# Transposing normalized keys and queries two units at a time, in halves of 64 rows, in a hybrid decoder layer

## The chip, the cores and the metric

The kernel runs on one core of a Trainium2 chip. The metric is the device time of one execution in microseconds. A core has TensorE (PE; its weight loads are listed apart as PEld), VectorE (DVE), ScalarE (ACT), GpSimd (POOL) and SyncE (SP), which here only issues DMAs. Each engine works through its own list of instructions in order; semaphores hold an instruction back until another engine or a DMA is done.

## The reference

One layer on x (2048 tokens, width 1024): an adaptive norm, one projection to queries, keys, values, forget logits and three conv inputs, attention of 8 heads of 64 beside a short gated convolution, an output projection, and a convolutional feed-forward part. What the change touches is the part that makes queries and keys:

```python
h = rmsnorm(x, norm1_g) * (1 + sc1) + sh1
proj = h @ w_in
q, k, v, fg, xin, bg, cg = jnp.split(proj, IN_SPLITS, axis=-1)
q = rmsnorm(q.reshape(b, s, ATTN_HEADS, HEAD_DIM), q_norm_g)
k = rmsnorm(k.reshape(b, s, ATTN_HEADS, HEAD_DIM), k_norm_g)
```

Keys and queries are wanted later with the head dimension on the partitions, so each normalized block of 128 tokens by 512 columns has to be transposed. They are also wanted as a pair of fp16 numbers, a high part and the rest (the low part), because products are made from three fp16 products.

## The kernel before

The work runs in stages: values and modulation, keys, queries, the conv inputs, attention with the output projection, and the feed-forward part. The change lies in the stage of keys and queries, `project` (L618). `project` is called for keys (L812) and then for queries (L814). Each call goes through 16 units of 128 tokens. I call them K0 to K15 and Q0 to Q15.

In a unit TensorE makes 24 matmuls of 128x512 (eight steps k of three fp16 products, `mm3`, L145) into a PSUM tile `acc`. ACT squares it (L649), DVE sums the squares per head and makes the reciprocal root (L651, L652, `rsqrt`), and DVE writes the normalized block `qn` (L655) to SBUF. `qn` goes onto a list, `normed`.

`finish(i, qn)` (L620) does the rest for one unit. TensorE transposes the block in four pieces of 128x128 fp32 (L623) into one PSUM tile `pt` of 512 columns. ACT scales and copies it to `tf` (L629), POOL makes the fp16 high part `th` (`pool_copy`, L139), DVE the low part `tl` (L631), and SP issues two stores to DRAM (L633). `finish` is called behind the last matmuls of a unit (`k == MID`, MID is 7) when three units are on the list, so it handles the block of three units earlier. The three units that are left at the end of a call are finished by `finish_last`: those of the keys as hooks of Q0, Q1 and Q2, those of the queries inside the first conv chunk (L854), one after each of the products x, c and b.

All PSUM tiles of this kind come from one pool, `ps_t`, with the tag `tr` and **two buffers**, taken in turn. Other small products take tiles of the same tag: the running offset `po` (L542, hook of K4), the scale of a weight group (`power_of_two`, a transpose at L173 and a matmul at L179, called from `next(group)` behind the last matmuls of a unit), `largest_value` and `value_scale` (L579, L584), and the modulation columns `pm` (L691, from `piece`, a hook of Q3, Q6, Q9, Q12 and Q15). The wrapper `K` keeps an instruction in program order on its engine. All TensorE instructions named here are wrapped, so on TensorE they stand just where the program has them: a small product that follows `finish` stands right behind its transposes, ahead of the next unit's matmuls. The other engines' lists are ordered by a scheduler.

During the queries a value tile is also split per unit (`value_tile`, L592): SP loads `vt` (L595), ACT and DVE make its high and low part `vo` (L600, L601), and SP stores them. `magnitudes` (L728) streams weights of the feed-forward part through ACT (L732). In SBUF, `tf` and `vt` share a tag with two buffers, and `th` and `vo` share another.

Of the kernel before, what the change touches and what calls it, by code (L numbers as in the profile page):

```python
# [20 lines left out]
P = 128  # L21
# [25 lines left out]
def kernel(  # L47
# [104 lines left out]
    with ExitStack() as ph:  # L152
# [438 lines left out]

        def value_tile(i):  # L592

            vt = bp.tile([P, AW], F32, tag="tf", name="vt")
            nc.sync.dma_start(vt, v_sc[i * P : (i + 1) * P, :])  # L595

            def split():
                vo = bp.tile([P, H, P], F16, tag="th", name="vo")
                v3 = vt.rearrange("p (h d) -> p h d", d=DH)
                A.activation(vo[:, :, 0:DH], v3, AF.Copy, scale=vs)  # L600
                V.scalar_tensor_tensor(vo[:, :, DH:P], v3, vs, vo[:, :, 0:DH], op0=ALU.mult, op1=ALU.subtract)  # L601
                nc.sync.dma_start(
                    v16_sc[:, i * P : (i + 1) * P, :, :].rearrange("r p a d -> p r a d"),
                    vo.rearrange("p (r a) d -> p r a d", a=2),
                )

            return split
# [7 lines left out]
                splits.append(value_tile(i))  # L615


        def project(w, units, col, gain, dst_hi, dst_lo, hooks, lull, group):  # L618

            def finish(i, qn):  # L620
                pt = ps_t.tile([P, 512], F32, tag="tr", name="pt")
                for j in range(4):
                    K(T.transpose(  # L623
                        pt[:, j * P : (j + 1) * P], qn[:, 2 * j : 2 * j + 2, :].rearrange("p h d -> p (h d)"), ident
                    ))
                tf = bp.tile([P, 512], F32, tag="tf", name="tf")
                th = bp.tile([P, 512], F16, tag="th", name="th")
                tl = bp.tile([P, 512], F16, tag="tl", name="tl")
                A.activation(tf, pt, AF.Copy, scale=gain)  # L629
                pool_copy(th, tf)  # L630
                V.tensor_tensor(tl, tf, th, op=ALU.subtract)  # L631
                for dst, src in ((dst_hi, th), (dst_lo, tl)):
                    nc.sync.dma_start(dst[:, :, i * P : (i + 1) * P], src.rearrange("p (j n) -> p j n", j=4))  # L633

            normed = []
            for i in range(NT):
                ch, t = divmod(i, 4)
                acc = ps_m.tile([P, 512], F32, tag="mm", name="acc")
                for k in range(KD):
                    ah, al = h_hi[k][ch][:, t * P : (t + 1) * P], h_lo[k][ch][:, t * P : (t + 1) * P]  # L640
                    mm3(acc, ah, al, w[k][0], w[k][1], k == 0, k == KD - 1)
                    if k == 3 and lull[0] <= i < lull[1]:
                        magnitudes()
                    if k == MID and len(normed) == 3:
                        finish(*normed.pop(0))
                next(group)
                a3 = acc.rearrange("p (h d) -> p h d", d=DH)
                sq = bp.tile([P, 512], F32, tag="z", name="sq")
                A.activation(sq, acc, AF.Square)  # L649
                r = bp.tile([P, 16], F32, tag="r", name="r")[:, 0:H]  # L650
                V.tensor_reduce(r, sq.rearrange("p (h d) -> p h d", d=DH), axis=AX.X, op=ALU.add)  # L651
                V.tensor_scalar(r, r, 1.0 / DH, units[1], op0=ALU.mult, op1=ALU.add)  # L652
                rsqrt(bp, r, H, "rq")
                qn = bp.tile([P, H, DH], F32, tag="qn", name="qn", bufs=4)
                V.tensor_tensor(qn, a3, r.unsqueeze(2).broadcast_to([P, H, DH]), op=ALU.mult)  # L655
                normed.append((i, qn))
                if i in hooks:
                    hooks[i]()
                if col == 0:
                    value_tiles(i)  # L660
                if lull[0] <= i < lull[1]:
                    magnitudes()

            def finish_last():
                finish(*normed.pop(0))
                if col == 0 and not normed:
                    value_tiles(NT)

            return finish_last
# [141 lines left out]
        w_q, u_q, group = columns_of(0, "wl")  # L811
        last_k = project(w_k, u_k, AW, gq[:, 1:2], k_hi, k_lo, {0: largest_gains, 1: gain_scales, 3: running_sum, 4: running_offset, 7: largest_value, 9: value_scale}, (0, 13), group)  # L812
        convs = [conv_group(0)]
        last_q = project(w_q, u_q, 0, gq[:, 0:1], q_hi, q_lo, {0: last_k, 1: last_k, 2: last_k, 3: piece, 6: piece, 9: piece, 12: piece, 15: piece}, (2, 15), convs[0][2])  # L814

        def load_head(h):

# [16 lines left out]
        for j in range(4):  # L834
# [5 lines left out]
            for ch in range(4):  # L840
# [7 lines left out]
                for name in ("x", "c", "b"):  # L848
                    pr[name] = ps_m.tile([P, 512], F32, tag="mm", name="pr")
                    for k in range(KD):  # L850
                        wh, wl = w[name][k // 4]
                        mm3(pr[name], wh[:, k % 4, :], wl[:, k % 4, :], h_hi[k][ch], h_lo[k][ch], k == 0, k == KD - 1)
                        if (j, ch, k) == (0, 0, MID):
                            last_q()  # L854
                    if j < 3 or (ch, name) == (0, "x"):
                        magnitudes()
# [16 lines left out]
                    next(scales)  # L873
                bt = bp.tile([P, 512], F32, tag="qn", name="bt", bufs=4)
                A.activation(bt, pr["b"], AF.Copy, scale=inv)
                y = bp.tile([P, 512], F32, tag="tf", name="y")
                cw = [cst[:, 72 + 4 * m + j : 73 + 4 * m + j] for m in range(3)]
                G.tensor_scalar(y, z[:, 0:512], cw[0], None, op0=ALU.mult)
                V.scalar_tensor_tensor(y, z[:, 1:513], cw[1], y, op0=ALU.mult, op1=ALU.add)
# [913 lines left out]
```

## Time and profile before

| what | value |
|---|---|
| median of 3 runs | 2374.75 us (2369.72 to 2375.34) |
| the profiled execution | 2379.02 us |
| its span in the trace | 2377.3 us |
| mean granted TensorE clock | 0.994 |
| transposes of the change's stage (L623), 128 of them | from 176.1 to 354.2 us |
| TensorE busy in the whole span | 96% |

The span is the time from the first to the last instruction; 1.7 us of the profiled execution lie around it. In the rows of the views, PE is TensorE's matmul side and PEld its weight loads. A form such as `128*128 128x512` gives rows and columns of the array in use, then the output's partitions by columns. A matmul's recorded duration holds its way through the array, so consecutive matmuls overlap in the record: their cost to TensorE is the distance between their starts. The idle time ahead of an instruction stands in brackets with what ended it.

### The profile page before, as it was taken

The page shows a single profiled execution, that of the slowest core. Times are in us where ns is not written, and L with a number is a line of the kernel's source. Part 1 is how long each engine was busy: PE and PEld are TensorE (multiplying, and loading weights), DVE is VectorE, ACT ScalarE, POOL GpSimd, SP SyncE. Part 2 cuts the span into 40 slices and gives each one's busy share as a digit, 9 for nine tenths or more (in the row PEclk, how much of TensorE's full clock was granted, in tenths as well). Part 3 has the DMA queues.
Part 4 walks back from the last instruction along what each step waited for, and adds up shares of the span by engine and source line. Part 5 has one row for each costly group of instructions (what it writes and reads, how often), then busy time and mean ns, then how long its engine had stood idle before and what let it go on. Part 6 is the DMA issues. An engine that isn't in the chain of part 4 may idle for free.

```text
span 2377.3 us, 38568 instructions
## 1 busy us (share of the span) xinstructions
PE 2277.8 (96%) x14208; PEld 1359.0 (57%) x14208; DVE 1740.6 (73%) x3404; ACT 1163.9 (49%) x1990; POOL 339.0 (14%) x282
## 2 busy tenths in 40 slices
PE   5899999999899898999999999999999999999998
PEld 5764554444677676444444444678764444447886
DVE  6768886673999887456999999766955566566556
ACT  5745543320788887343556556465522232224332
POOL 0211111111677784001000000000000000000000
PEclk9999999999999999999999999999999999999999
DMA  9346699963899997434465556676654444446665
GB/s 285 135 156 174 165 263 300 299 214 84 164 182 190 196 188 150 166 111 168 169 216 196 207 210 215 235 235 224 224 185 161 145 158 147 150 164 209 220 204 194
DMA packets 452646, 455.25 MB, mean 191 GB/s; under 512 B 191248, under 2 KB 301160, under 8 KB 451432
## 3 DMA queue, kind: packets, MB, share of 16 engines
q1 hardware_dynamic: 445336, 435.94, 62.0%
q10 hardware_dynamic: 4752, 8.46, 1.0%
q0 software_dynamic: 2368, 8.39, 0.9%
q8 instruction: 111, 1.82, 0.3%
q14 instruction: 79, 0.65, 0.1%
HBM read 284.84 MB, written 134.28 MB: 176 GB/s over the span
## 4 chain that ended last, share of the span: by engine, by line
PE 78%; DVE 11%; DMA 4%; ACT 4%; issue 2%; SPq 1%; POOL 0%; DVEq 0%; ACTq 0%
PE acc L1591 28%; PE acc L1748 14%; PE acc L145 13%; PE pr L145 10%; PE pv L145 2%; PE pt L1107 2%; PE ps L1046 1%; DMA far<-wide 1%; PE ps L1047 1%; DVE near L1114 1%; PE po L1143 1%; DVE s_t L1070 1%; ACT s_t L1087 1%; PE po L1145 1%; PE po L1144 1%
## 5 line engine op out<-in xcount | busy, mean ns | idle before, releaser
L1591 PEld LDWEIGHTS <-pair 128*128 128x128 f16 x3696 | 361.5, 98 | 439.7 <-issue 5.0
L1591 PE MATMUL acc<-t,pair 128*128 128x512 f16 x2112 | 477.3, 379 | 1.9 <-DVE t L1426 1.9
L1591 PE MATMUL acc<-b,pair 128*128 128x512 f16 x1584 | 363.4, 379 | 0.0
L1515 DVE TENSOR_TENSOR lo<-raw,hi 128x1024 fp32r<-128x1024 f32 x154 | 186.8, 1223 | 137.5 <-ACT hi L1514 128.3
L1604 DVE SCALAR_TENSOR_TENSOR w<-w,fcw,w 128x1024 f32<-128x1024 f32 x176 | 226.1, 1285 | 79.4 <-ACT w L1599 73.2
L1514 ACT ACTIVATE hi<-raw 128x1024 fp32r<-128x1024 f32 x154 | 160.9, 1056 | 188.7 <-PE acc L1748 136.4
L1748 PE MATMUL acc<-lo,hi 128*128 128x512 f32 x616 | 242.9, 394 | 7.3 <-DVE lo L1515 7.2
L1748 PE MATMUL acc<-hi 128*128 128x512 f32 x616 | 244.8, 397 | 5.4 <-DVE u L1426 3.6
L1748 PE MATMUL acc<-hi,lo 128*128 128x512 f32 x616 | 242.3, 393 | 0.0
L145 PEld LDWEIGHTS <-h 128*128 128x128 f16 x1344 | 130.3, 98 | 97.5 <-DVE h L358 5.4
L1599 ACT ACTIVATE w<-w,fcw 128x1024 f32<-128x1024 f32 x88 | 100.6, 1143 | 160.7 <-DVE w L1426 160.7
L145 PE MATMUL acc<-wp,mp 128*128 128x512 f16 x768 | 171.1, 382 | 1.1 <-DVE raw L999 1.0
L1087 ACT ACTIVATE s_t<-s_t,nb,cst 128x2048 f32<-128x2048 f32 (+15 forms) x128 | 164.7, 1288 | 4.8
L1099 POOL TENSOR_TENSOR wide<-s_t,wide 128x1024 f16<-128x1024 f32 x64 | 136.8, 2137 | 5.3
L1748 PEld LDWEIGHTS acc<-lo,hi 128*128 128x128 f32 x616 | 117.1, 190 | 33.3 <-DVE lo L1515 9.5
L1748 PEld LDWEIGHTS acc<-hi 128*128 128x128 f32 x616 | 117.0, 190 | 32.4 <-DVE u L1426 5.7
L1070 DVE CUSTOM_DVE_ANT_0 s_t<-ps,nf,mx 128x512 f32<-128x512 f32 (+1 forms) x192 | 119.4, 643 | 16.5 <-PE ps L1049 8.2
L1748 PEld LDWEIGHTS acc<-hi,lo 128*128 128x128 f32 x616 | 117.1, 190 | 24.9
L145 PE MATMUL pr<-h,wh 128*128 128x512 f16 x576 | 126.5, 379 | 0.0
L145 PEld LDWEIGHTS <-mp 128*128 128x128 f16 x768 | 75.3, 98 | 88.9 <-issue 3.5
L145 PE MATMUL pr<-h,wl 128*128 128x512 f16 x576 | 125.8, 379 | 0.0
L1046 PE MATMUL ps<-kh,qs 128*128 128x512 f16 (+1 forms) x320 | 109.6, 347 | 5.5 <-DVE mx L1070 4.5
(362 smaller groups left out, 4084.8 us busy)
## 6 DMA issues: line engine op xcount, KB each, us to landing
up_sc<-pair SPq DMA_DIRECT2D x132, 256.0 KB, 2.7
pair<-up_sc SPq DMA_DIRECT2D x132, 256.0 KB, 3.0
wx<-in_w_up_dram SPq DMA_DIRECT2D x88, 256.0 KB, 3.6
raw<-in_w_up_dram SPq DMA_DIRECT2D x44, 512.0 KB, 3.7
y_t<-t SPq DMA_DIRECT2D x88, 256.0 KB, 2.6
raw<-y_t SPq DMA_DIRECT2D x88, 256.0 KB, 3.9
raw<-w_sc SPq DMA_DIRECT2D x88, 256.0 KB, 4.4
y_b<-y SPq DMA_DIRECT2D x66, 256.0 KB, 2.0
```

The source lines that it names most:

```text
L145: ins = T.matmul(acc, lhsT=a, rhs=b, start=st, stop=sp)
L1046: K(T.matmul(ps[:, 0:cw], lhsT=qt, rhs=kh[:, c0 : c0 + cw], start=True, stop=False))
L1070: K(V.tensor_tensor_reduce(out=s_t[:, o0 + c0 : o0 + c0 + cw], in0=ps[:, 0:cw], in1=nf[:, c0 : c0 + cw], scale=1.0, scalar=-3.0e38 if g == ...
L1087: K(A.activation(cols, cols, AF.Exp, bias=nb[:, p : p + 1], scale=qk[:, 4:5], accum_out=un["l"][:, p : p + 1]))
L1099: K(G.tensor_tensor(wide[:, 1, :], s_t[:, WB * P : WU], wide[:, 0, :], op=ALU.subtract))
L1107: K(T.transpose(pt[:, b * P : (b + 1) * P], s_t[:, (b0 + b) * P : (b0 + b + 1) * P], ident))
L1514: K(A.activation(hi, raw, AF.Copy))
L1515: K(V.tensor_tensor(lo, raw, hi.bitcast(F32), op=ALU.subtract))
L1591: K(T.matmul(acc, lhsT=a, rhs=b, start=st, stop=sp, skip_group_check=True))
L1599: K(A.activation(y, u[:, 0:1024], AF.Copy, scale=fcw[:, ct : ct + 1]))
L1604: K(V.scalar_tensor_tensor(y, u[:, m : m + 1024], fcw[:, m * 44 + ct : m * 44 + ct + 1], y, op0=ALU.mult, op1=ALU.add))
L1748: K(T.matmul(acc[t], lhsT=a[:, c], rhs=b, start=st, stop=sp, skip_group_check=True))
```

## The change

`finish` takes two blocks, of units i and i+1, at once. Each 128x128 transpose becomes two, one of the upper and one of the lower 64 tokens: 64 rows of `qn` by 128 columns against a 64x64 part of the identity. The upper halves go to one PSUM tile and the lower halves to another, so a call takes both buffers of `tr`. That is 16 transposes of 128x64 where there were two times four of 128x128. ACT copies in four pieces of 256 columns, and the copy, the low part and the two stores then run once on 1024 columns. `finish` is called when four units are on the list (K4, K6 to K14, and the same for Q); the two last pairs of the keys are finished behind the matmuls of Q0 and Q1 (`others`), those of the queries behind the products x and c. `tf` and `tl` have one buffer, `vt` gets a tag of its own with one buffer, and the conv stage's `y` takes the tag `th`.

```diff
--- before.py
+++ after.py
@@ -591,7 +591,7 @@
 
         def value_tile(i):
 
-            vt = bp.tile([P, AW], F32, tag="tf", name="vt")
+            vt = bp.tile([P, AW], F32, tag="vt", name="vt", bufs=1)
             nc.sync.dma_start(vt, v_sc[i * P : (i + 1) * P, :])
 
             def split():
@@ -615,22 +615,30 @@
                 splits.append(value_tile(i))
 
 
-        def project(w, units, col, gain, dst_hi, dst_lo, hooks, lull, group):
-
-            def finish(i, qn):
-                pt = ps_t.tile([P, 512], F32, tag="tr", name="pt")
-                for j in range(4):
-                    K(T.transpose(
-                        pt[:, j * P : (j + 1) * P], qn[:, 2 * j : 2 * j + 2, :].rearrange("p h d -> p (h d)"), ident
-                    ))
-                tf = bp.tile([P, 512], F32, tag="tf", name="tf")
-                th = bp.tile([P, 512], F16, tag="th", name="th")
-                tl = bp.tile([P, 512], F16, tag="tl", name="tl")
-                A.activation(tf, pt, AF.Copy, scale=gain)
+        def project(w, units, col, gain, dst_hi, dst_lo, hooks, lull, group, others={}):
+
+            def finish():
+                pair = [normed.pop(0) for _ in range(2)]
+                i = pair[0][0]
+                rows = slice(0, 64), slice(64, P)
+                pts = [ps_t.tile([P, 512], F32, tag="tr", name="pt").rearrange("p (e j n) -> p e j n", e=2, n=64) for _ in rows]
+                for e, (_, qn) in enumerate(pair):
+                    for j in range(4):
+                        for pt, rw in zip(pts, rows):
+                            K(T.transpose(
+                                pt[:, e, j, :], qn[rw, 2 * j : 2 * j + 2, :].rearrange("p h d -> p (h d)"), ident[rw, rw]
+                            ))
+                tf = bp.tile([P, 1024], F32, tag="tf", name="tf", bufs=1)
+                th = bp.tile([P, 1024], F16, tag="th", name="th")
+                tl = bp.tile([P, 1024], F16, tag="tl", name="tl", bufs=1)
+                t4 = tf.rearrange("p (j e n) -> p e j n", j=4, e=2)
+                for pt, rw in zip(pts, rows):
+                    for e in range(2):
+                        A.activation(t4[:, e, :, rw], pt[:, e], AF.Copy, scale=gain)
                 pool_copy(th, tf)
                 V.tensor_tensor(tl, tf, th, op=ALU.subtract)
                 for dst, src in ((dst_hi, th), (dst_lo, tl)):
-                    nc.sync.dma_start(dst[:, :, i * P : (i + 1) * P], src.rearrange("p (j n) -> p j n", j=4))
+                    nc.sync.dma_start(dst[:, :, i * P : (i + 2) * P], src.rearrange("p (j n) -> p j n", j=4))
 
             normed = []
             for i in range(NT):
@@ -641,8 +649,10 @@
                     mm3(acc, ah, al, w[k][0], w[k][1], k == 0, k == KD - 1)
                     if k == 3 and lull[0] <= i < lull[1]:
                         magnitudes()
-                    if k == MID and len(normed) == 3:
-                        finish(*normed.pop(0))
+                    if k == MID and len(normed) == 4:
+                        finish()
+                    if k == MID and i in others:
+                        others[i]()
                 next(group)
                 a3 = acc.rearrange("p (h d) -> p h d", d=DH)
                 sq = bp.tile([P, 512], F32, tag="z", name="sq")
@@ -662,7 +672,7 @@
                     magnitudes()
 
             def finish_last():
-                finish(*normed.pop(0))
+                finish()
                 if col == 0 and not normed:
                     value_tiles(NT)
 
@@ -811,7 +821,7 @@
         w_q, u_q, group = columns_of(0, "wl")
         last_k = project(w_k, u_k, AW, gq[:, 1:2], k_hi, k_lo, {0: largest_gains, 1: gain_scales, 3: running_sum, 4: running_offset, 7: largest_value, 9: value_scale}, (0, 13), group)
         convs = [conv_group(0)]
-        last_q = project(w_q, u_q, 0, gq[:, 0:1], q_hi, q_lo, {0: last_k, 1: last_k, 2: last_k, 3: piece, 6: piece, 9: piece, 12: piece, 15: piece}, (2, 15), convs[0][2])
+        last_q = project(w_q, u_q, 0, gq[:, 0:1], q_hi, q_lo, {3: piece, 6: piece, 9: piece, 12: piece, 15: piece}, (2, 15), convs[0][2], {0: last_k, 1: last_k})
 
         def load_head(h):
 
@@ -850,7 +860,7 @@
                     for k in range(KD):
                         wh, wl = w[name][k // 4]
                         mm3(pr[name], wh[:, k % 4, :], wl[:, k % 4, :], h_hi[k][ch], h_lo[k][ch], k == 0, k == KD - 1)
-                        if (j, ch, k) == (0, 0, MID):
+                        if (j, ch, k) == (0, 0, MID) and name != "b":
                             last_q()
                     if j < 3 or (ch, name) == (0, "x"):
                         magnitudes()
@@ -873,7 +883,7 @@
                     next(scales)
                 bt = bp.tile([P, 512], F32, tag="qn", name="bt", bufs=4)
                 A.activation(bt, pr["b"], AF.Copy, scale=inv)
-                y = bp.tile([P, 512], F32, tag="tf", name="y")
+                y = bp.tile([P, 512], F32, tag="th", name="y")
                 cw = [cst[:, 72 + 4 * m + j : 73 + 4 * m + j] for m in range(3)]
                 G.tensor_scalar(y, z[:, 0:512], cw[0], None, op0=ALU.mult)
                 V.scalar_tensor_tensor(y, z[:, 1:513], cw[1], y, op0=ALU.mult, op1=ALU.add)
```

On TensorE, in unit Q4. `h_1_834` is the last of eight normalized inputs, `wl` the weights of the queries, `pt` the PSUM tile of tag `tr`, `qn` a normalized block, and L173 the transpose that starts the scale of a weight group. Before:

```order
L145 MATMUL acc<-wl,h_1_834 128x512
L623 MATMUL pt<-ident,qn 128x128 [waits DVE_49,Activation_49]
L623 MATMUL pt<-ident,qn 128x128 x3
L173 MATMUL pt<-ident,group 1x128 [waits Activation_49]
L145 LDWEIGHTS h_1_820
```

And now:

```order
L145 MATMUL acc<-wl,h_1_834 128x512
L628 MATMUL pt<-ident,qn 128x64 [waits DVE_49,PE_49,Activation_49]
L628 MATMUL pt<-ident,qn 128x64 [waits PE_49,Activation_49]
L628 MATMUL pt<-ident,qn 128x64 x6
L628 MATMUL pt<-ident,qn 128x64 [waits DVE_49]
L628 MATMUL pt<-ident,qn 128x64 x7
L173 MATMUL pt<-ident,group 1x128 [waits PE_49,Activation_49]
L145 LDWEIGHTS h_1_820
```

Before, the four transposes fill one buffer and L173 takes the other, whose last reader was the ACT copy of the unit before. Now the sixteen fill both buffers, so the ACT copy that L173 waits for is that of the sixteen transposes just ahead of it. The same holds at three more places, where a call of `finish` and a small product meet in one unit: K4 (L542), Q6 (L179) and Q12 (L701, L691 before).

On ACT, around unit K4 (`wx` are the streamed weights, `sq` the square of a unit's result, `tf` the copy of the transposed block, `nf_sc` the running sum's store), the difference reads:

```order
+L742 ACTIVATE wx,l_2065<-wx 128x512 x2
+L659 ACTIVATE sq<-acc 128x512
+L637 ACTIVATE tf<-pt,gq 128x4x64 x4
 L547 DMA nf_sc<-cum 128x128
-L732 ACTIVATE wx,l_2065<-wx 128x512 x2
-L649 ACTIVATE sq<-acc 128x512
-L629 ACTIVATE tf<-pt,gq 128x512
```

One copy of 512 columns behind each unit's square has become four copies of 256 columns (4 runs of 64) behind every second unit's square.

## The prediction

> **What bounds the kernel now.** I read the page's totals and chain first, then the busy time of the stages that hold the change, then the groups of this stage.
>
> ```profile
> span 2377.3 us, 38568 instructions
> PE 2277.8 (96%) x14208; PEld 1359.0 (57%) x14208; DVE 1740.6 (73%) x3404; ACT 1163.9 (49%) x1990; POOL 339.0 (14%) x282
> ...
> PE 78%; DVE 11%; DMA 4%; ACT 4%; issue 2%; SPq 1%; POOL 0%; DVEq 0%; ACTq 0%
> ```
>
> ```profile
> core 0: us, PE busy (x) PEld busy (x) DVE busy (x) ACT busy (x) POOL busy (x), PEclk, DMA share, GB/s
> 170.00:266.00 96.00, 95.48 (x479) 47.95 (x477) 81.77 (x324) 45.50 (x106) 9.93 (x16) 1.00 0.59 157
> 266.00:362.00 96.00, 96.00 (x485) 48.62 (x484) 80.89 (x280) 50.73 (x113) 11.86 (x19) 1.00 0.89 253
> 362.00:500.00 138.00, 138.00 (x654) 64.91 (x653) 98.60 (x206) 45.45 (x109) 15.76 (x18) 1.00 0.94 302
> ```
>
> TensorE is busy for all but 0.5 us from 170 to 500 us, at full clock. So in the stage of keys and queries, and in the conv stage behind it, time is TensorE's: what its list loses or gains there moves the end by as much, and ACT (half busy) or DVE matter only where TensorE waits for them. The view of groups for 170 to 362 us holds what the change replaces, and a weight load that is used below:
>
> ```profile
> L631 DVE TENSOR_TENSOR tl<-tf,th 128x512 f16<-128x512 f32 x32 | 22.0, 687 | 3.4 <-POOL th L139 3.4
> L629 ACT ACTIVATE tf<-pt,gq 128x512 f32<-128x512 f32 x32 | 21.8, 681 | 5.6 <-DVE tl L631 4.2 <-DVE rqt L130 1.0 <-DVE rqy L127 0.3
> L623 PE MATMUL pt<-ident,qn 128*128 128x128 f32 x128 | 19.2, 273 | 0.0
> ...
> L179 PEld LDWEIGHTS pt<-group,ones 1*128 1x128 f32 x4 | 0.6, 182 | 0.3 <-issue 0.3
> ```
>
> **The change part by part.** *Removed: 128 transposes.* One unit in the timeline, TensorE's rows:
>
> ```profile
> 199.26 0.60 PE L623 MATMUL pt<-ident,qn 128*128 128x128 f32 x4
> ...
> 200.69 0.27 PE L579 MATMUL pt<-ident,vm 128*1 128x128 f32 x1 [0.52 <-ACT tf L629]
> 200.79 5.34 PE L145 MATMUL acc<-wh,h 128*128 128x512 f16 x24
> 205.97 0.60 PE L623 MATMUL pt<-ident,qn 128*128 128x128 f32 x4
> 206.41 3.83 PE L145 MATMUL acc<-wh,h 128*128 128x512 f16 x17
> ```
>
> 24 matmuls take 205.97 - 200.79 = 5.18 us, 0.216 each; the four transposes take 206.41 - 205.97 = 0.44 us, 0.109 each, although each is recorded with 273 ns. So the 128 transposes are worth 128 x 0.109 = **14.0 us** of TensorE's time, and that is all there is to win in them.
>
> *Added: 16 groups of 16 half transposes.* Two things have to be priced. First, the height of the array in use changes from 128 rows to 64 and back. The trace has such a change only where a matmul of one or two rows stands between others; here TensorE's rows, then the weight loads:
>
> ```profile
> 503.76 0.59 PE L145 MATMUL pr<-h,wh 128*128 128x512 f16 x2
> 504.28 0.38 PE L179 MATMUL pt<-group,ones 1*128 1x1 f32 x2
> 504.59 0.82 PE L145 MATMUL pr<-h,wh 128*128 128x512 f16 x3
> ```
>
> ```profile
> 504.28 0.29 PEld L179 LDWEIGHTS pt<-group,ones 1*128 1x128 f32 x2 [0.42 <-DVE mo L686]
> ```
>
> The second L145 starts at 503.76 + 0.216 = 503.98 and is through at 504.19. L179 starts at 504.28, 0.09 us later. From 504.19 to the next L145 at 504.59 are 0.40 us. The two weight loads take about 0.11 us each (0.29 together, less the 0.18 of the last one's own record). That leaves about 0.19 for the two changes of height, 0.09 into and 0.10 out of it. A row with columns 128*1 (L579, above) goes into L145 without such a gap: 200.79 - 200.69 is the 0.109 of its 128 columns.
>
> Second, the half transposes themselves:
>
> ```profile
> 931.68 0.33 PE L1107 MATMUL pt<-ident,s_t 128*128 128x128 f32 x1 [0.64 <-ACT tm L1163]
> ...
> 931.88 0.19 PE L1144 MATMUL po<-v,far 128*128 128x64 f16 x1
> 931.90 0.19 PE L1145 MATMUL po<-v,far 128*128 128x64 f16 x1
> 931.93 0.81 PE L145 MATMUL acc<-wp,mp 128*128 128x512 f16 x3
> ```
>
> The fp32 transpose behind an idle stretch lasts 0.33 us in place of 0.27, so its weight load shows 0.06 us. Its 128 columns stream in 0.109, so 64 columns take 0.055. Each half still loads 128 columns of weights, 0.06, which hides under the other 0.055 or barely shows. Matmuls of 64 columns, each with its load, stand 0.03 apart (931.88, 931.90, 931.93), so issue allows 16 in 0.46. If both halves of the array work at once, 8 steps of 0.06 give 0.46 to 0.48; if one after the other, 16 x 0.055 to 0.06 gives 0.9; if no load hides either, 16 x 0.109 = 1.75. No row here shows two halves at work together. The Trainium skill, "TensorEngine Tiling (Array Packing)", Key Properties, says that different tiles can load weights and multiply in parallel. I take 0.50, near the issue rate of the 64-column rows, with the first load exposed (0.06) and the two changes of height (0.19): 0.75 a group, 16 x 0.75 = 12.0. **Transposes: 12.0 - 14.0 = -2.0 us.** Bounds: 16 x 0.46 = 7.4 with changes of height free, -6.6; halves in turn, 16 x 1.15 = 18.4, +4.4; nothing hidden, 16 x 2.0 = 32, +18.
>
> A rule of the skill speaks against it: "TensorE: Matmul & The Clock Gate", section "LDWEIGHTS (loading the stationary operand)", has a load's time set by its columns alone, columns / 1.2 in ns, so 107 ns for each half however few its rows. By it a group would be 8 x 0.107 = 0.86 instead of 0.50, and the sum 16 x 0.36 = 5.8 us higher. The 0.06 of L1107 disagrees; the trace decides.
>
> *Added: four waits for ACT.* At K4, Q4, Q6 and Q12 a small product follows the transposes and needs one of the two buffers that they have just filled. Behind it on TensorE stand the next unit's 24 matmuls and everything after. ACT's rows, for the copy behind a transpose and for two copies of about 256 columns in a row:
>
> ```profile
> 199.95 0.68 ACT L629 ACTIVATE tf<-pt,gq 128x512 f32<-128x512 f32 x1
> ```
>
> ```profile
> 88.38 0.47 ACT L469 ACTIVATE vt<-pv,scales 128x260 f32<-128x260 f32 x1
> 88.74 0.46 ACT L470 ACTIVATE vt<-pv,scales 128x252 f32<-128x252 f32 x1
> ```
>
> ACT starts 0.09 us after the recorded end of the transposes (199.26 + 0.60 = 199.86). Two pieces, which free the first buffer, take 0.36 + 0.46 = 0.82. TensorE goes on 0.06 after that (L629 ends at 200.63, L579 starts at 200.69). The recorded end lies 0.273 - 0.109 = 0.16 after the point at which TensorE could have gone on, and 0.10 of that is already paid as the change of height: 0.16 + 0.09 + 0.82 + 0.06 - 0.10 = 1.03 us, four times 4.1. At Q12 ACT is late in the trace:
>
> ```profile
> 319.61 0.60 PE L623 MATMUL pt<-ident,qn 128*128 128x128 f32 x4
> 320.04 0.51 PE L691 MATMUL pm<-ones,mo 128*128 128x1 f32 x4
> ...
> 321.53 0.67 ACT L629 ACTIVATE tf<-pt,gq 128x512 f32<-128x512 f32 x1
> ```
>
> The copy starts 321.53 - 320.21 = 1.32 us after the transposes instead of 0.09, which TensorE did not feel since L691 took the other buffer. Now it would: 1.2 more. **Waits: +5.3 us.** Bounds: half of it, if ACT overlaps the pieces, and about 12 if it is late at the other places too.
>
> *Removed: one wait.* In unit K7 three users of the two buffers met, and L579 waited 0.52 us for the copy (row above). Now K7 has no `finish`, so L179 and L579 find buffers that were read a unit ago: **-0.5 us.**
>
> *At nothing.* ACT's four pieces cost about 3 x 0.36 + 0.46 = 1.5 us a pair where two copies cost 1.4; DVE and POOL run once on 1024 columns. All of it lies beside the 11 us that TensorE needs for two units, and TensorE reads none of their results before attention. The stores on SP are half as many; behind them in SP's list stand the loads of `vt`, `wx` and the conv weights, which gain rather than lose. `vt` with one buffer waits for DVE's `vo`, as it did when it took turns with `tf`. A block is transposed three units after its second unit ended, as before, so DVE has the same time for `qn`. If that cover went, TensorE would wait ahead of L628 for DVE, which the trace does not show ahead of L623 (idle 0.0).
>
> Sum: -2.0 + 5.3 - 0.5 = +2.8 us, so 2381.8 against the profiled 2379.02. The median of the runs shown is 4.3 below that execution, and with the same difference it becomes 2374.75 + 2.8 = **2377.6 us**.
>
> **The rivals.** 0.3% of this kernel is 7.1 us, about what a measurement can tell from no change.
>
> *The halves work in turn (25%, slower).* The change then doesn't do what it says: one half's load or stream holds the other's, a group costs 0.9 + 0.25 = 1.15. For it: each half still loads 128 columns. Against it: loads already hide under 64-column matmuls in attention, 0.03 apart. +4.4 + 5.3 - 0.5 = +9.2, 2384.0. It decides from a group of about 1.02 us on: 16 x (1.02 - 0.874) + 4.8 = 7.1.
>
> *ACT late at the waits (13%, slower).* ACT's list holds the value split, which waits for its load:
>
> ```profile
> ACT vo L600 <- DMA vt<-v_sc: 21.9, 12, 4.0
> ```
>
> 12 waits of up to 4.0 us, mean 1.8, all in the queries, where three of the four places lie. Against it: ACT was on time at Q4 and Q6. Two of the three at 4.0 in place of Q12's 1.2 give 4.1 + 8.0 = 12.1, and with -2.0 - 0.5 the sum is +9.6, 2384.4. It decides once the four waits sum to 9.6 us.
>
> *Faster (7%).* The halves overlap, 64 rows change height for nothing (-6.6), and the waits vanish because ACT copies while the last transposes run: -6.6 - 0.5 = -7.1, 2367.7. Against it: L579's wait shows that a copy of a full buffer is felt.
>
> **How the numbers follow.** The forecast, +2.8 us, has 55%. The range goes from 2369, where transposes come near their lower bound (-5.7), to 2389: halves in turn (+4.4) with waits of 9 (+9 - 0.5) give 2387.7, and 1.3 is for the spread of the runs. The case in which no load hides (+18 and more) is left out, as is most of the faster one. Faster by over 0.3%: 7%. Within 0.3%: 55%. Slower: 25% + 13% = 38%.
>
> **What would show it.** In the profile after: the half transposes (form 64*128) 0.03 apart and a group's first start to the next L145 0.6 to 0.7 us; a gap of about 0.09 ahead of each group; four waits of TensorE for ACT's `tf`, near 1 us, and near 2 at Q12; none at K7. The first product of the conv stage should start 2 to 4 us later than now. A group of 1 us or more makes the first rival right; waits over 3 us the second. I am wrong altogether if TensorE waits somewhere else, ahead of L628 for DVE or in the conv stage for its weights.

## The result and the profile after

| | before | after |
|---|---|---|
| median | 2373.42 us (2369.72 to 2375.34, 4 runs) | 2384.49 us (2382.38 to 2387.20, 4 runs) |
| profiled execution, its span | 2379.02, 2377.3 us | 2387.20, 2385.5 us |
| mean granted TensorE clock | 0.994 | 0.992 |

The ratio is 1.0043, with a 95% interval of 1.0031 to 1.0054: the change makes the kernel slower by 11 us, and the whole interval lies above the 0.3% that the prediction took as the limit of what can be told from no change. That lies inside the range of the prediction, but not in its likeliest case. It is the time that the second rival gave, "ACT late at the waits" (2384.4). All ratios here are of fast runs; three slow ones, two of e10 (3386 and 4719 us) and one of e11 (6091 us), stand in the medians of those two experiments.

The page of the changed kernel, span, totals and the chain:

```profile
span 2385.5 us, 38772 instructions
PE 2279.2 (96%) x14336; PEld 1354.1 (57%) x14336; DVE 1744.7 (73%) x3388; ACT 1169.0 (49%) x2022; POOL 336.6 (14%) x266
...
PE 73%; DVE 15%; DMA 4%; ACT 4%; issue 3%; SPq 1%; POOL 0%; DVEq 0%; ACTq 0%; POOLq 0%
```

The totals hardly tell that anything happened: TensorE is busy for 2279.2 us in place of 2277.8, in a span that is 8.2 us longer. The busy time by stretch tells where. The same three stretches as in the prediction:

```profile
170.00:266.00 96.00, 95.07 (x545) 44.76 (x544) 83.92 (x315) 46.51 (x118) 8.38 (x8) 1.00 0.52 155
266.00:362.00 96.00, 86.72 (x475) 40.62 (x474) 79.59 (x275) 51.67 (x128) 7.37 (x8) 0.93 0.82 248
362.00:500.00 138.00, 138.00 (x666) 64.77 (x665) 94.69 (x194) 46.89 (x110) 18.10 (x19) 1.00 0.91 288
```

In the queries (266 to 362 us) TensorE is now idle for 96.00 - 86.72 = 9.28 us, where it was idle for none, and the granted clock is 0.93 in place of 1.00. Both are losses, and they add up.

For a measure that leaves out the other stages I take the distance from the first matmul of the keys to the last product of the conv stage, between TensorE's starts. Rows of before, its first keys and its last conv products:

```profile
155.08 2.75 PE L145 MATMUL acc<-wh,h 128*128 128x512 f16 x12
...
588.67 5.99 PE L145 MATMUL pr<-h,wl 128*128 128x512 f16 x27
```

And of after:

```profile
156.34 1.46 PE L145 MATMUL acc<-wh,h 128*128 128x512 f16 x6
...
593.25 15.70 PE L145 MATMUL pr<-h,wl 128*128 128x512 f16 x72
```

A row of 27 has its last start 26 x 0.2157 us behind its first: 588.67 + 5.61 - 155.08 = 439.2 before, and with 71 x 0.2157 for the row of 72, 593.25 + 15.31 - 156.34 = 452.2 after. **The stretch is 13.0 us longer.** Calculated from the single starts it is 439.21 and 452.23; so are the stretches below. Attention begins 1.41 us behind the stretch in both. The spans differ by 8.2 only, since attention and the following stages were shorter in this execution of after; that part is not the change's, as the last experiment shows.

**The half transposes.** One group that meets no small product, TensorE's rows (in the form `64*128 64x64` the last part is the moving operand, 64 rows by 64 columns; the output is 128x64):

```profile
229.77 0.71 PE L628 MATMUL pt<-ident,qn 64*128 64x64 f32 x16
230.42 1.04 PE L145 MATMUL acc<-wh,h 128*128 128x512 f16 x4
```

From the group's first start to the next L145 are 0.65 us, and ahead of it is a gap of 0.09 (the last L145 starts 0.310 before it, and takes 0.216). That makes 0.74 a group, where the two times four transposes took 2 x 0.437 = 0.874: 16 x 0.134 = **-2.2 us**, as forecast (-2.0).

**The four waits.** What TensorE waited for from 170 to 366 us (in total, times, longest), all of it:

```profile
PE pm L701 <- ACT tf L637: 6.0, 1, 6.0
PE pt L179 <- ACT tf L637: 2.0, 1, 2.0
PE pt L173 <- ACT tf L637: 1.3, 1, 1.3
PE po L542 <- ACT tf L637: 0.9, 1, 0.9
```

They are the four places of the forecast: Q12, Q6, Q4 and K4. Their sum is 10.2 us where 5.3 were forecast, and the wait of K7 is gone (-0.5). The largest, at Q12, reads in the timeline (the queue's row is the load's issue):

```profile
324.46 0.55 SPq L595 DMA_DIRECT2D vt<-v_sc  x1
324.57 0.71 PE L628 MATMUL pt<-ident,qn 64*128 64x64 f32 x16
...
328.04 0.72 ACT L600 ACTIVATE vo<-vt,vs 128x512 f16<-128x512 f32 x1 [4.04 <-DMA vt<-v_sc]
328.67 0.61 ACT L742 ACTIVATE wx<-wx 128x512 f32<-128x512 f32 x1
...
329.28 0.61 ACT L742 ACTIVATE wx<-wx 128x512 f32<-128x512 f32 x1
...
329.89 0.57 ACT L659 ACTIVATE sq<-acc 128x512 f32<-128x512 f32 x1
...
330.37 1.55 ACT L637 ACTIVATE tf<-pt,gq 128x256 f32<-128x256 f32 x4
...
331.24 1.01 PE L701 MATMUL pm<-ones,mo 128*128 128x1 f32 x4 [5.95 <-ACT tf L637]
```

The transposes end at 325.28. ACT stands at the value split, 4.04 us for a load issued at 324.46, then does two pieces of the streamed weights and a square that were due before, and comes to the copy 330.37 - 325.28 = 5.1 us late. Two pieces later L701 starts. In before the same copy was late by 1.3 us, and nobody waited for it.

**What was not foreseen: the clock.** Stretches at and behind the waits of Q6 and Q12 (length, then busy time and count of PE, PEld, DVE, ACT, POOL, then the granted clock):

```profile
290.30:293.70 3.40, 3.40 (x10) 1.20 (x9) 3.06 (x14) 1.89 (x5) 1.04 (x1) 0.50 0.43 142
293.70:297.10 3.40, 3.40 (x17) 1.57 (x16) 3.09 (x11) 0.55 (x1) 0.00 (x0) 1.00 0.55 164
324.60:327.90 3.30, 0.69 (x17) 0.55 (x16) 2.73 (x14) 0.00 (x0) 0.00 (x0) 0.99 1.01 277
327.90:331.20 3.30, 0.00 (x0) 0.00 (x0) 2.21 (x4) 3.16 (x9) 0.00 (x0) 0.50 1.00 324
331.20:338.10 6.90, 6.86 (x19) 3.00 (x20) 6.14 (x21) 2.67 (x7) 1.05 (x1) 0.50 0.96 287
338.10:345.00 6.90, 6.90 (x34) 3.13 (x33) 5.32 (x21) 2.54 (x6) 0.00 (x0) 1.00 0.87 258
```

Behind the wait of 1.98 us the clock is at 0.50 for 3.4 us, in which 10 matmuls run in place of 17. Behind that of 5.95 us it is at 0.50 for another 6.9 us of work: 19 in place of 34. The loss is half of these times, 1.7 + 3.4 = **5.1 us**, and no idle row shows it.

Together: -2.2 - 0.5 + 10.2 + 5.1 = +12.6 of the 13.0. The -2.2 carries the price of the groups that meet no small product over to all 16; measured as a whole (e9) the transposes win 1.85, and the sum is then 12.95.

### The profile page after: what moved, and what is told of

Read it like the earlier page. It is cut to its first block, busy times and chain, and to the rows that moved or that the text cites. A ratio compares the mean times of both kernels' runs of the same rounds, so it can differ in the third digit from the quotient of the medians.

```text
span 2385.5 us, 38772 instructions
## 1 busy us (share of the span) xinstructions
PE 2279.2 (96%) x14336; PEld 1354.1 (57%) x14336; DVE 1744.7 (73%) x3388; ACT 1169.0 (49%) x2022; POOL 336.6 (14%) x266
## 3 DMA queue, kind: packets, MB, share of 16 engines
q8 instruction: 112, 1.84, 0.3%
## 4 chain that ended last, share of the span: by engine, by line
PE 73%; DVE 15%; DMA 4%; ACT 4%; issue 3%; SPq 1%; POOL 0%; DVEq 0%; ACTq 0%; POOLq 0%
PE acc L1601 28%; PE acc L1758 14%; PE pr L145 10%; PE acc L145 9%; PE pv L145 2%; PE pt L1117 2%; PE ps L1056 1%; PE ps L1057 1%; DVE near L1124 1%; PE po L1153 1%; DMA far<-wide 1%; DVE s_t L1080 1%; PE po L1155 1%; PE po L1154 1%; DVE t L1436 1%
## 5 line engine op out<-in xcount | busy, mean ns | idle before, releaser
L145 PEld LDWEIGHTS <-h 128*128 128x128 f16 x1344 | 130.7, 99 | 103.6 <-issue 6.1
L145 PE MATMUL acc<-wp,mp 128*128 128x512 f16 x768 | 169.4, 379 | 1.1 <-DVE raw L1009 1.0
L145 PE MATMUL pr<-h,wh 128*128 128x512 f16 x576 | 126.4, 379 | 0.0
L145 PE MATMUL pr<-h,wl 128*128 128x512 f16 x576 | 125.8, 379 | 0.0
L145 PEld LDWEIGHTS <-mp 128*128 128x128 f16 x768 | 74.9, 98 | 87.7 <-issue 1.3
```

Source lines behind the costliest of these rows:

```text
L145: ins = T.matmul(acc, lhsT=a, rhs=b, start=st, stop=sp)
```

## The experiments

Theory A: the loss is the four waits and the half clock behind them, and the half transposes bring what was forecast. It has to be told from a loss in the half transposes themselves. Of ACT's lateness there were two theories: V, the value split's load is late because `vt` has one buffer, so the load of a unit is only issued when DVE has made `vo` of the last; and R, `vo` waits for the buffers that it shares with `th`.

The results first. Each ratio is against runs of before on the same chip, with its 95% interval; the stretch is that of above, from one profile each. Differences to the change are between medians of different chips, on which before itself differs by up to 1.5 us (2373.42 to 2374.88).

| run | median us | ratio | stretch us | TensorE's waits in the stretch, us |
|---|---|---|---|---|
| before | 2373.42 | 1 | 439.21 | 0.5 |
| the change | 2384.49 | 1.0043 (1.0031 to 1.0054) | 452.23 | 10.2, and 5.1 by the clock |
| e1 | 2377.92 | 1.0014 (1.0006 to 1.0023) | 446.57 | 7.4 at L628 |
| e2 | 2379.59 | 1.0025 (1.0015 to 1.0034) | 449.51 | 8.0 |
| e3 | 2384.28 | 1.0040 (1.0026 to 1.0054) | 450.01 | 8.2 |
| e4 | 2370.81 | 0.9987 (0.9978 to 0.9996) | 438.62 | none |
| e5 | 2377.39 | 1.0022 (1.0013 to 1.0031) | 444.35 | 5.4 |
| e6 | 2375.88 | 1.0004 (0.9996 to 1.0013) | 441.85 | 3.2 at L628 |
| e7 | 2388.27 | 1.0066 (1.0052 to 1.0080) | 455.07 | 11.3 at L628 |
| e8 | 2368.96 | 0.9984 (0.9975 to 0.9993) | 438.62 | none |
| e9 | 2371.55 | 0.9986 (0.9976 to 0.9995) | 436.77 | none |
| e10 | 2375.43 | 1.0002 (0.9993 to 1.0012) | 438.61 | none |
| e11 | 2371.62 | 0.9991 (0.9981 to 1.0000) | 437.56 | none |
| e12 (one run) | 2370.59 | | 439.21 | 0.5 |

**e1, the small products in a pool of their own.** In the changed kernel, `po`, `pm`, `pc` and the two tiles of a weight group's scale take buffers of the pool `ps_m`, so that they meet no transposes.

```diff
-                po = ps_t.tile([P, 512], F32, tag="tr", name="po")
+                po = ps_m.tile([P, 512], F32, tag="mm", name="po")
...
-            chain = power_of_two(ps_t, m, rw, top)
+            chain = power_of_two(ps_m, m, rw, top, "mm")
```

> The change, with the small products (running offset, weight scales, modulation columns) in the pool of the unit results, which has six buffers, instead of the two buffers that the half transposes fill. Theory A (the loss is TensorE's waits for ACT at K4, Q4, Q6 and Q12, 10.5 us in the trace, and about 5 us of half clock behind the long ones): no wait of TensorE for the copy is left, no half clock between 280 and 340 us, and the time is 2 to 3 us below the kernel before. Theory B (the waits are not what costs; half transposes with their changes of height, or the copies, low parts and stores in blocks of 1024 columns, do): within 3 us of the change, some 8 to 11 us above before.

Measured: 2377.92, 6.6 below the change, but 3.0 above before, where 2 to 3 below it were expected. The waits at the small products are gone. In their place the transposes wait, behind the end of the queries; TensorE's waits from 170 to 366 us, and two rows of the timeline:

```profile
PE pt L628 <- ACT tf L637: 7.4, 4, 6.0
```

```profile
351.17 0.72 ACT L600 ACTIVATE vo<-vt,vs 128x512 f16<-128x512 f32 x1 [5.71 <-DMA vt<-v_sc]
...
354.21 1.55 ACT L637 ACTIVATE tf<-pt,gq 128x256 f32<-128x256 f32 x4
...
355.08 0.36 PE L628 MATMUL pt<-ident,qn 64*128 64x64 f32 x1 [6.03 <-ACT tf L637]
```

Where TensorE no longer waits for ACT, it also no longer lets ACT catch up. In the queries the copy begins 0.6, 3.0, 6.5, 6.6, 8.0, 10.5 and 10.4 us behind its transposes, pair by pair, until the last two pairs have to wait for the buffers; from 352.6 on, inside that wait, the clock is at one half for 6.8 us. So the place of the wait was one thing and ACT's lateness another, and moving the places does not cure the second.

**e2, one meeting less** (a unit less in which a small product follows the transposes). `piece` moves from Q12, where a pair is transposed, to Q13, where none is.

```diff
-        last_q = project(w_q, u_q, 0, gq[:, 0:1], q_hi, q_lo, {3: piece, 6: piece, 9: piece, 12: piece, 15: piece}, (2, 15), convs[0][2], {0: last_k, 1: last_k})
+        last_q = project(w_q, u_q, 0, gq[:, 0:1], q_hi, q_lo, {3: piece, 6: piece, 9: piece, 13: piece, 15: piece}, (2, 15), convs[0][2], {0: last_k, 1: last_k})
```

> The change with the fourth modulation step moved from Q12 to Q13, where no transposes are made; the other three meetings stay. Theory A: the wait of 6.0 us at Q12 and the half clock behind it (about 3.4 us lost) go, so about 9 us below the change and 1 to 3 us above before. Theory B: no different from the change by more than 1 us.

Measured: 2379.59, 4.9 below the change, where about 9 were expected. The 5.95 became waits of 0.81 and 1.71 at L701 and, at the last pairs, 0.38 and 1.47 at L628; two half-clock stretches of 3.4 us remain. The lateness finds the next place, as in e1.

**e3, the same pairs with whole transposes.** Eight transposes of 128x128, a unit to each buffer; copy, low part and stores stay as changed.

```diff
-                        for pt, rw in zip(pts, rows):
-                            K(T.transpose(
-                                pt[:, e, j, :], qn[rw, 2 * j : 2 * j + 2, :].rearrange("p h d -> p (h d)"), ident[rw, rw]
-                            ))
+                        K(T.transpose(pts[e][:, j, :], qn[:, 2 * j : 2 * j + 2, :].rearrange("p h d -> p (h d)"), ident))
```

> The change with eight transposes of 128x128 in place of sixteen halves, one unit to each buffer; the copy in four pieces of 256 columns, the low part, the stores and the order stay. Theory A: a group costs about 0.87 us of TensorE in place of 0.74, 16 x 0.13 = 2 us above the change, with the four waits as they are. Theory B with the halves to blame: 5 us or more below the change, since the changes of height are gone.

Measured: 2384.28, the same as the change, with a stretch 2.2 us shorter. What TensorE waited for:

```profile
PE pm L698 <- ACT tf L634: 6.5, 1, 6.5
PE pt L179 <- ACT tf L634: 0.6, 1, 0.6
PE pt L173 <- ACT tf L634: 0.5, 1, 0.5
PE po L542 <- ACT tf L634: 0.5, 1, 0.5
```

The loss is there without a single half transpose, so it is not theirs. The short waits are shorter here, 0.55 in place of 0.93 at K4. Whole transposes fill the first buffer with the first unit, half a group earlier, so its copy can begin before the group is through; the halves fill both buffers at the group's end. That is worth 0.4 us where ACT is on time. Since the waits differ, this run can't price the halves; e10 does.

**e4, the small products' pool in before.** The edit of e1 in the kernel before.

> The kernel before, with its small products in the pool of the unit results as well. Theory A: only the wait at K7 goes, 0.5 us below before, so within 1 us of it. A rival for the first run (that pool is better in itself, whatever the transposes do): this kernel gains as much as the first run gains against before.

Measured: 2370.81, ratio 0.9987. The wait of K7 is gone and the stretch is 0.6 shorter, as the -0.5 of the prediction has it. The median is lower by more than that. Where the rest comes from no profile shows.

**e5, two buffers for `vt`.** In the changed kernel; one buffer of `ws` pays for it in SBUF.

```diff
-            vt = bp.tile([P, AW], F32, tag="vt", name="vt", bufs=1)
+            vt = bp.tile([P, AW], F32, tag="vt", name="vt", bufs=2)
...
-                t = lp.tile([P, 512], F32, tag="ws", name="ws", bufs=6)
+                t = lp.tile([P, 512], F32, tag="ws", name="ws", bufs=5)
```

> The change with two buffers for the value tile's load (and five in place of six for the down weights' sums, for the room). Theory V (ACT is late with its copies because the value split behind which they queue waits for its load, and with one buffer that load is issued only after the unit before is split): ACT's waits for this load shrink from 21 us to a few, the copies are on time, the four waits of TensorE become about 1 us each as forecast, no half clock is left there, and the time is 7 to 9 us below the change, about 1 to 3 above before. Theory R (it is the tag that the high part shares with the split's output): no different from the change by more than 2 us.

Measured: 2377.39, 7.1 below the change and 3.8 above before. TensorE's waits:

```profile
PE pm L701 <- ACT tf L637: 1.8, 1, 1.8
PE pt L179 <- ACT tf L637: 1.0, 1, 1.0
PE po L542 <- ACT tf L637: 0.9, 1, 0.9
PE pt L173 <- ACT tf L637: 0.9, 1, 0.9
PE pt L628 <- DVE qn L665: 0.8, 1, 0.8
```

The row of ACT's waits for this load, in the changed kernel:

```profile
ACT vo L600 <- DMA vt<-v_sc: 21.2, 7, 4.5
```

It does not occur any more in e5. ACT waits in the value split for others:

```profile
ACT vo L600 <- DMA q_hi<-th: 10.8, 3, 4.2
ACT vo L600 <- DVE tl L639: 7.7, 3, 3.1
```

`th` and `vo` share a tag, and that is theory R's wait; but the copies of the queries are on time up to Q12 (0.04 to 0.9 us late), so it does no harm there. Not all of ACT's lateness is the load's: in the keys, from K6 to K10, the copies start 4 to 4.7 us late in the change and 4.1 to 4.4 in e5, where no small product follows, and behind Q12 they are up to 4.2 late in e5. This run is the forecast's kernel: the four waits are 0.93, 0.93, 0.99 and 1.77, 4.6 in all for 5.3, and the time is 3.8 above before for 2.8. One half-clock stretch of 3.4 us is left, behind the 1.77.

**e6, e1 and e5 together.** Both edits in the changed kernel.

> Both: small products in the pool of the unit results, and two buffers for the value tile's load. Theory V: the copies' lateness, which grew to 10 us in the first run, stays under 3 us, TensorE waits nowhere from the keys to the conv stage, and that stretch is 16 x 0.135 = 2 us shorter than with the kernel before and its small products moved (438.6 us): 436.5. The time: 2 us below that kernel, 4 to 6 below before. Theory R: as the first run, with the wait of 6 us at the last pair.

Measured: 2375.88, equal to before (1.0004). There are waits at one place only:

```profile
PE pt L628 <- DVE qn L665: 1.7, 1, 1.7
PE pt L628 <- ACT tf L637: 1.5, 2, 1.1
```

That is the last pair of the queries, at 347 to 350 us. It stands behind product c, 24 matmuls or 5.2 us behind the pair at x, where other pairs are 11 us apart; neither the copy of the pair before nor `qn` of Q15 is done. The half clock follows there, too, for 3.4 us.

**e7, theory R by itself.** The edit of e1, one buffer of `vt`, and a tag of two buffers for `vo` (and the conv stage's `y`); `th` keeps one, `ws` has five.

```diff
-                vo = bp.tile([P, H, P], F16, tag="th", name="vo")
+                vo = bp.tile([P, H, P], F16, tag="vo", name="vo")
...
-                th = bp.tile([P, 1024], F16, tag="th", name="th")
+                th = bp.tile([P, 1024], F16, tag="th", name="th", bufs=1)
```

> The first run with tags of their own for the high part (one buffer) and the split's output (two buffers); the value tile's load keeps one buffer. Theory V: the copies are still late by several us at the end of the queries, and TensorE still waits at the last pair. Theory R: the lateness and that wait are gone, as expected of the run with two buffers by the other theory.

Measured: 2388.27, the slowest of all, with seven waits of L628 for the copy:

```profile
PE pt L628 <- ACT tf L637: 10.1, 7, 5.9
PE pt L628 <- DVE qn L665: 1.2, 1, 1.2
```

Buffers for `vo` did not help, so R is not borne out. The test is not clean, though, since `th` lost a buffer in it, and what that alone costs was not measured.

**e8, both edits in before.**

> The kernel before with small products moved and two buffers, under a tag of its own, for the value tile's load. TensorE waits nowhere in this stage of the kernel before, so by theory V nothing changes against the kernel before with its small products moved (2370.8), within 1.5 us. A rival: two buffers are better in themselves, and it gains as much as they bring in the change.

Measured: 2368.96, ratio 0.9984, the lowest time of all, but its stretch is that of e4 (438.62). ACT waits for `vt` in before as well (21.9 us in 12 waits), and it costs TensorE nothing there, since between two users of a buffer lies a whole unit.

**e9, the change without its waits.** e6, and the last two pairs behind x and b instead of x and c.

```diff
-                        if (j, ch, k) == (0, 0, MID) and name != "b":
+                        if (j, ch, k) == (0, 0, MID) and name != "c":
```

> As the run with small products moved and two buffers for the value tile's load, and the last two pairs of the queries finished behind the conv products x and b, two units apart, in place of x and c, one unit apart. If the waits are the whole loss, none is left from the keys to the conv stage, no half clock there, and that stretch takes 438.6 - 16 x 0.135 = 436.5 us; the time is 2 us below the same form of the kernel before (2369.0), near 2367. If pairs cost TensorE something that the groups' own record does not show, it stays at 438 or above.

Measured: a stretch of 436.77 (436.5 expected), no wait of TensorE in it and full clock:

```profile
170.00:266.00 96.00, 96.00 (x549) 45.20 (x548) 84.59 (x315) 49.58 (x125) 8.38 (x8) 1.00 0.55 163
266.00:362.00 96.00, 96.00 (x554) 45.79 (x553) 80.80 (x268) 52.04 (x131) 8.28 (x10) 1.00 0.84 257
```

The stretch is 1.85 us shorter than e8's, and that is what the change is worth when nothing waits. The time is 2371.55, ratio 0.9986, about 3 us below before; this is not the change's alone, since e8, with the two other edits and without the change, is as far below (0.9984), and the intervals of the two ratios are nearly the same. Nor is ACT on time in e9: at the last two pairs the copy starts 6.5 and 7.7 us late, but nothing on TensorE needs the buffers before.

**e10, e9 with whole transposes**, the edit of e3 in e9.

> The same with eight transposes of 128x128 in place of sixteen halves. Halves at once: 16 x 0.135 = 2.2 us more in the stretch, 438.6, the same as with one unit at a time. If the halves' changes of height cost more than they bring: less than the run with halves.

Measured: a stretch of 438.61, 1.84 longer than e9's, for an expected 2.2. A group of eight, and one of e9's:

```profile
218.53 1.04 PE L627 MATMUL pt<-ident,qn 128*128 128x128 f32 x8
219.40 0.81 PE L145 MATMUL acc<-wh,h 128*128 128x512 f16 x3
```

```profile
216.60 0.71 PE L628 MATMUL pt<-ident,qn 64*128 64x64 f32 x16
217.25 0.61 PE L145 MATMUL acc<-wh,h 128*128 128x512 f16 x2
```

0.87 against 0.65 + 0.09. With waits gone on both sides, this is the price of the halves alone, and theory A's part on them holds.

**e11, four upper halves and then four lower ones**, meant to make the halves work in turn, in e9.

```diff
-                    for j in range(4):
-                        for pt, rw in zip(pts, rows):
+                    for pt, rw in zip(pts, rows):
+                        for j in range(4):
```

> As the run with no waits, but the four upper halves of a unit first and then its four lower halves, so neighbours in TensorE's list use the same half of the array. If the halves in the change work at once: 16 half transposes take 16 x 0.055 to 0.06 = 0.87 to 0.96 us in place of 0.49, a group about 1.15 and the stretch 16 x 0.4 = 6 us longer. If they never did: no difference.

Measured: a stretch of 437.56, 0.8 longer than e9's, where 6 were expected. The group:

```profile
216.22 0.77 PE L628 MATMUL pt<-ident,qn 64*128 64x64 f32 x16
216.93 0.39 PE L145 MATMUL acc<-wh,h 128*128 128x512 f16 x1
```

The edit did not do what it was meant to. In e9 the single starts come in pairs 3 to 4 ns apart, a pair every 62 ns (0, 3, 113, 117, 175, 178, 238, 242 ns and so on, eight pairs in 0.49 us). In e11 they still come in pairs, 4 to 13 ns apart, a pair or a single one every 62 ns, nine of them in 0.545 us. So two half transposes run at a time in both orders, and they are one of each half, which the semaphores of the records show. In e11's program, of a group's first eight transposes only the first and the fifth (the first lower one) wait for another engine's semaphore; of the last eight, the twelfth (the last upper one) and the sixteenth raise TensorE's own. In the trace, in all 16 groups, the weight load that starts second carries the wait of the fifth, and the transpose that starts fifteenth the raise of the twelfth. So TensorE itself took lower halves ahead of upper ones that stand before them in its list. The 0.8 in the stretch is about 16 times the 0.053 us that a group takes longer. What a group costs whose halves do work in turn stays unmeasured.

**e12, before once more**, one run with a profile.

> The kernel before, unchanged, for a second profile: whether its attention stage again takes 336.2 us with two waits of 2.2 us for a transposed load, or 332 to 333 as in the variants' profiles. By chance: the second profile shows 332 to 334. By the kernel: 336 again.

Measured: the stretch is 439.21 again, to 0.01. From the first matmul of attention to the end it is another matter: attention took 334.27 us where the first profile of the same kernel has 336.24, and the feed-forward stage 1252.37 for 1257.98. What the change's profile seemed to win there (332.34 in attention) is within what two executions of one kernel differ by, or near it. It is not counted for the change.

## Why the prediction was right in its range and wrong in its likeliest case

- *The bound.* Right. What TensorE's list gains or loses in this stage moves the end: the stretches of e9 and e10 differ by 1.84 us, about what their 16 groups differ by (2.1).
- *Transposes, -2.0.* Right: 0.74 a group for 0.75, -1.85 in all (e9); and the halves work two at a time (e11), 62 ns a pair for the 60 that were taken. The first rival falls. The Trainium skill's "TensorEngine Tiling (Array Packing)", Key Properties, that tiles can work in parallel, agrees with the rows. Its rule that was weighed against the change (the Trainium skill, "TensorE: Matmul & The Clock Gate", section "LDWEIGHTS (loading the stationary operand)", columns / 1.2 in ns, so 107 a load) does not hold for these: 16 loads lie in 0.49 us, two every 62 ns.
- *K7, -0.5.* Right. No wait is left there, and e4 gives 0.6 for the same wait alone.
- *Four waits, +5.3.* **This is the step that failed.** The places were right, and so was the price of a wait with ACT on time: 0.93 at K4 for 1.03. The lateness was taken as that of before, 1.2 at Q12 and none elsewhere. It was 5.1 at Q12, 1.1 at Q6 and 0.5 at Q4: waits of 5.95, 1.98 and 1.35. Behind it stands the sentence "`vt` with one buffer waits for DVE's `vo`, as it did when it took turns with `tf`", which put that edit at nothing. With two buffers (e5) the four waits are 4.6, near the forecast. The row of 12 waits of up to 4.0 us had been read, and given to a rival of 13%: its price (four waits of over 9.6) is what came.
- *The clock, not in the sum.* A stall was priced at its length. Two of the four brought a half-clock stretch, 5.1 us, nearly the waits' whole forecast. No term of the sum, nor of a rival, holds it.
- *Stores, DVE and POOL at nothing.* Right in the changed kernel: TensorE waits there for nothing but `tf`. In e2, e5, e6 and e7 it does wait 0.8 to 1.7 us for DVE's `qn` ahead of L628, in the first three at the end of the queries, so that cover is thin at the last pairs.
- *The range, by luck.* Its upper end was built from halves in turn (+4.4) with waits of 9, and the rival's 2384.4 from waits of 12.1. The halves did not work in turn, the waits are 10.2, the clock adds 5.1 that nobody forecast, and the median rose by 11.1 where the stretch rose by 13.0. The rival had the mechanism; that its number fits to 0.1 us is luck.

So the loss is settled: waits for a late ACT copy and the clock behind them; without them the same transposes win 1.85 us (e9 against e8, e10). That ACT's lateness at Q4, Q6 and Q12 came from the single buffer of `vt` is shown by e5. Which part theory R has, and why the medians of e4 and e8 are lower by 3 to 4 us with 0.6 of it in the stretch, stays open.

## What to carry to other kernels

When a change takes all buffers of a ring at once, every other user of that ring becomes a wait for the reader's whole backlog: price it from how late that reader may be by its own list, not from how late it was while nobody waited. Taking a waiting place away (e1, e2) only moves the backlog on to the next place; the cure is at what makes the reader late (e5), and then at the places (e6, e9). Where stalls of TensorE that lie within 3.4 us of each other add up to some 1.7 us, they are to be priced with a possible half-clock stretch of 3.4 us, too, half of which is lost.

## What the runs showed of the hardware that was not expected

- The clock falls at short stalls. The waits of 1.98 us (the change), 1.77 (e5), 1.71 (e2) and 1.47 (e2, with 0.38 two us ahead) were each followed by 3.4 us at 0.50; that of 1.74 us in Q6 of e2 was not, nor any of up to 1.35 us that stood alone. At the long waits the half clock began inside the wait and outlasted it by 6.9 us (5.95, the change), 4.4 (6.03, e1), 5.0 (6.5, e3) and 5.9 (5.90, e7).
- What decides is the idle time within one window of a fixed grid. In each trace all the switches of the clock down to one half lie whole multiples of 3.413 us apart. With the span cut at these points, each full-clock window from 150 to 610 us, in all 14 traces, was followed by half clock when the idle time of TensorE's matmul rows in it was 1.71 us or more (10 windows), and none was with up to 1.68 us. The 1.74 us of e2 lie across a border, 1.53 of them in one window; the 1.71 lie whole in one. In e6 and e7 several waits in one window count together: 2.68 us in e6, where the longest wait is 1.67, and 2.25 in e7, where it is 1.79. In the other stages it went either way from 1.71 to 1.94 us. The Trainium skill, "TensorE: Matmul & The Clock Gate", Part 1, has the clock halved after at least one idle window of about 3.4 us, and the window running free. The grid agrees with that; that a whole window has to be idle, these runs do not bear out: half of one was enough.
- Half transposes of 64 rows and 64 columns in fp32 run two at a time, a pair in 62 ns, whether the program alternates the halves or gives four of each in a row (0.49 and 0.545 us for 16); in the second case TensorE takes them in another order than its list has them (e11).
- The change of the height in use cost 0.09 us ahead of each of the 12 groups that stand between rows of L145, as estimated from the rows of L179.
